# The four sums of weight blocks of each Strassen pair: from VectorE to GpSimd

## The chip, the cores and the metric

The kernel runs on one core of a Trainium2 chip. The metric is device time in microseconds (us), the median of several executions. TensorE (PE in the profile) multiplies matrices, VectorE (DVE), ScalarE (ACT) and GpSimd (POOL) compute element by element, and SyncE (SP) issues most DMAs. Each engine works through its own queue in a fixed order: an instruction that waits holds up everything behind it on its engine.

## The reference, cut to what matters

One decoder layer on 256 tokens of width 2048 in float32: a mixer, a cross-attention, a SwiGLU feed-forward part of width 5632, and norms. Only the last part is touched:

```
def swiglu(h, w_gate, w_up, w_down):
    return (jax.nn.silu(h @ w_gate) * (h @ w_up)) @ w_down
...
        h = h + swiglu(rmsnorm(h, norm_ffn[i]), w_gate[i], w_up[i], w_down[i])
    return rmsnorm(h, norm_final)
```

## The kernel before, in words

**Chunks.** All weights stream through the core once, in one order (`plan`), in chunks of 128 partitions x 1024 elements: two blocks of 128 rows by 512 columns side by side. SP loads a chunk into one of 6 raw tiles (`r`, line 185). ACT rounds it to a high part `h` (line 224, 4 tiles), DVE subtracts to get a low part `l` (line 225, 4 tiles). PE multiplies with both: each product is three matmuls, high x high, low x high and high x low (lines 298, 299, 302). So PE is fed by a chain of load, ACT cast, DVE subtraction, and an `h` tile is free for the next chunk when PE has used it.

**Strassen pairs.** Some chunks are taken two at a time. The first, `g`, and the second, `u`, form a 2 x 2 arrangement of weight blocks, and with a 2 x 2 arrangement of activation blocks the product takes seven block products in place of eight (`seven_mm`, lines 1179, 1180, 1182). For it `pair_sums` makes four sums of weight blocks (lines 199 to 202). Line 199 adds the first halves of `g` and `u`, line 200 changes the first half of `u` in place, line 201 reads the result of 199, and line 202 reads that of 201 and overwrites the first half of `g`, so it must also wait until ACT and DVE have split `g`. Three of the results are then split into high and low parts as well (line 206 on ACT, line 207 on DVE); the fourth is the changed half of `u`, which is split with the rest of `u` on lines 224 and 225.

There are 28 pairs: 16 in the gate and up products (about 813 to 1147 us of the profile), 6 in the first half of the down product (1252 to 1345 us) and 6 in its second half (1359 to 1460 us). Within a part four to six ordinary chunks stand between two pairs. The sums of activation blocks for the down pairs (`token_sums`, lines 1155 to 1160, split on 1165 and 1166) are also made by DVE and ACT, some time ahead.

**What sets the order.** PE's and SP's instructions stand as the code is written. DVE's, ACT's and GpSimd's are put in order when the kernel is built, by a scheduler that goes by its own estimates of how long each instruction takes; so an edit to one instruction can move others in the queues of all three. `split_to` is called up to two chunks ahead of what PE is given.

Of the kernel before, what the change touches and what calls it, by code (L numbers as in the profile page):

```python
# [20 lines left out]
ALU = mybir.AluOpType  # L21
# [100 lines left out]
def trunk(tc, wst, vecs, xp, xtp, mp, mtp, wdt_in, nfin, outp):  # L122
# [9 lines left out]
    with ExitStack() as ctx:  # L132
# [18 lines left out]
        def nm(s):  # L151
            cnt[0] += 1
            return f"{s}{cnt[0]}"

        def slot(shape=(128, 512), dt=F32):
            return sp.tile(list(shape), dt, tag="s", name=nm("s"))
# [12 lines left out]
        tt = nc.vector.tensor_tensor  # L169
        ts = nc.vector.tensor_scalar  # L170
        stt = nc.vector.scalar_tensor_tensor
        gtt = nc.gpsimd.tensor_tensor
# [20 lines left out]
        def pair_sums(key, u):  # L193


            g = held.pop(key)
            a, b = slice(0, 512), slice(512, 1024)
            f = bp.tile([128, 1024], F32, tag="b", name=nm("b"))
            tt(f[:, a], g[:, a], u[:, a], ALU.add)  # L199
            tt(u[:, a], u[:, a], u[:, b], ALU.add)  # L200
            tt(f[:, b], f[:, a], u[:, b], ALU.add)
            tt(g[:, a], f[:, b], g[:, b], ALU.add)  # L202
            pair_parts[key] = []
            for x in (f[:, a], f[:, b], g[:, a]):
                h, l = slot(dt=F32R), slot(dt=F32R)
                nc.scalar.copy(h, x)  # L206
                tt(l, x, h.bitcast(F32), ALU.subtract)  # L207
                pair_parts[key].append((h, l))

        def split_to(n):  # L210
            while nsplit[0] < min(n, len(plan)):
                i = nsplit[0]
                key, w = plan[i]
                r = raws.pop(i)
                if key in first_of:
                    held[key] = r
                elif key in second_of:
                    pair_sums(second_of[key], r)
                h = hip.tile([128, 1024], F32R, tag="h", name=nm("h"))
                l = lop.tile([128, 1024], F32R, tag="l", name=nm("l"))  # L220
                m = 2 if i in (0, 2) else 1
                for j in range(m):
                    c = slice(j * w // m, (j + 1) * w // m)
                    nc.scalar.copy(h[:, c], r[:, c])  # L224
                    tt(l[:, c], r[:, c], h[:, c].bitcast(F32), ALU.subtract)  # L225
                los[i] = l
                his[i] = h
                nsplit[0] += 1
# [1261 lines left out]
```

## Time and profile before

| | before |
|---|---|
| median of 3 runs | 1490.93 us (1490.48 to 1491.18) |
| the profiled execution | 1491.33 us, span of its instructions 1489.6 us |
| PE busy | 1478.4 us, 99% |
| DVE busy | 1109.9 us, 75%, 1528 instructions |
| ACT busy | 829.6 us, 56% |
| GpSimd busy | 34.4 us, 2%, 46 instructions, nearly all before 550 us |
| mean granted TensorE clock | 0.999 |

The span runs from the first instruction to the last, and the execution's own time is 1.7 us more. A busy PE says that matmuls were in flight, and here they follow each other without a gap through the feed-forward part.

### The profile page before, as it was taken

The numbers are of one execution on the slowest core, as the hardware profiler recorded it, in microseconds if no ns is written. First come the engines' busy times: TensorE is split into PE (matmuls) and PEld (weight loads), VectorE is DVE, ScalarE is ACT, GpSimd is POOL, SyncE is SP. The second block draws the span as 40 slices with busy tenths as digits, with TensorE's granted clock in tenths as the row PEclk, the third lists the DMA queues.
The fourth block names the chain that finished last, engine by engine and source line by source line (L and its number), as shares of the span: only waits on it lengthen the run. The fifth ranks groups of instructions, "written<-read, shape, count | busy, mean of one in ns | idle before, by whom it ended". The sixth has DMA issues, their size and how long they took to land.

```text
span 1489.6 us, 18607 instructions
## 1 busy us (share of the span) xinstructions
PE 1478.4 (99%) x6649; PEld 1218.6 (82%) x6649; DVE 1109.9 (75%) x1528; ACT 829.6 (56%) x1155; POOL 34.4 (2%) x46
## 2 busy tenths in 40 slices
PE   9999999999999999999999999999999999999997
PEld 7788888888888888888888888888888888888886
DVE  6677777776785774665577788888887667979975
ACT  7476554857664554554465555555554444655553
POOL 0012000100000000000000000000000000000000
PEclk9999999999999999999999999999999999999999
DMA  9886766868767665876647676756766666765553
GB/s 368 267 286 223 279 214 221 292 223 303 241 212 275 217 233 193 283 274 213 249 166 236 239 242 205 245 204 209 238 226 241 225 220 198 242 217 194 202 187 110
DMA packets 149214, 346.71 MB, mean 233 GB/s; under 512 B 11360, under 2 KB 62976, under 8 KB 149120
## 3 DMA queue, kind: packets, MB, share of 16 engines
q1 hardware_dynamic: 140064, 338.64, 66.1%
q10 hardware_dynamic: 9056, 6.87, 1.5%
q8 instruction: 52, 0.85, 0.2%
q14 instruction: 42, 0.34, 0.1%
HBM read 321.30 MB, written 24.17 MB: 232 GB/s over the span
## 4 chain that ended last, share of the span: by engine, by line
PE 98%; DMA 0%; issue 0%; SPq 0%; ACT 0%; DVE 0%; DVEq 0%; POOLq 0%; POOL 0%
PE a L298 29%; PE a L299 29%; PE a L302 29%; PE m L1182 2%; PE m L1180 2%; PE m L1179 2%; PE a L1179 1%; PE a L1182 1%; PE a L1180 1%; PE m L719 1%; PE m L299 0%; PE m L298 0%; PE m L302 0%; DMA r<-in_w_dram 0%; PE m L1026 0%
## 5 line engine op out<-in xcount | busy, mean ns | idle before, releaser
L225 DVE TENSOR_TENSOR l<-r,h 128x1024 fp32r<-128x1024 f32 (+1 forms) x539 | 652.4, 1218 | 262.3 <-ACT h L224 253.0
L224 ACT CAST h<-r 128x1024 fp32r<-128x1024 f32 (+1 forms) x539 | 563.4, 1049 | 488.1 <-PE a L299 349.3
L298 PE MATMUL a<-h,s 128*128 128x512 f32 x1887 | 738.2, 391 | 1.0 <-ACT h L224 1.0
L299 PE MATMUL a<-h,s 128*128 128x512 f32 x1887 | 734.5, 389 | 0.0
L302 PE MATMUL a<-l,s 128*128 128x512 f32 x1887 | 507.4, 389 | 0.0
L298 PEld LDWEIGHTS a<-h,s 128*128 128x128 f32 x1887 | 354.3, 188 | 76.5 <-ACT h L224 2.1
L302 PEld LDWEIGHTS a<-l,s 128*128 128x128 f32 x1887 | 354.2, 188 | 73.8
L299 PEld LDWEIGHTS a<-h,s 128*128 128x128 f32 x1887 | 354.4, 188 | 72.6
L206 ACT CAST s<-b 128x512 fp32r<-128x512 f32 x56 | 33.9, 619 | 21.0 <-DVE b L199 17.2
L317 DVE STREAM_TRANSPOSE b<-s 128x512 f32<-128x512 f32 x62 | 40.6, 690 | 6.4 <-ACT s L324 6.4
L207 DVE TENSOR_TENSOR s<-b,s 128x512 fp32r<-128x512 f32 x56 | 37.9, 687 | 0.0
L660 DVE SCALAR_TENSOR_TENSOR t<-t,vec,t 128x255 f32<-128x255 f32 (+2 forms) x72 | 33.1, 492 | 3.4 <-ACT t L657 2.7
L199 DVE TENSOR_TENSOR b<-r,r 128x512 f32<-128x512 f32 x28 | 19.3, 689 | 17.3 <-DMA r<-in_w_dram 17.2
L324 ACT ACTIVATE s<-a,xr 128x512 f32<-128x512 f32 x42 | 26.4, 681 | 3.6 <-PE a L302 3.6
L1116 DVE TENSOR_TENSOR f<-a,f 128x512 f32<-128x512 f32 x32 | 20.6, 685 | 8.4 <-PE a L302 8.4
L1143 ACT CAST s<-f 128x512 fp32r<-128x512 f32 x22 | 13.6, 620 | 18.0 <-DMA f<-w 18.0
L1182 PE MATMUL m<-s,t 128*128 128x512 f32 x56 | 21.8, 389 | 0.0
L1179 PE MATMUL m<-s,t 128*128 128x512 f32 x56 | 21.8, 389 | 0.0
L1180 PE MATMUL m<-s,t 128*128 128x512 f32 x56 | 21.8, 389 | 0.0
L206 ACT CAST s<-r 128x512 fp32r<-128x512 f32 x28 | 17.3, 619 | 6.5 <-DVE r L202 6.3
L200 DVE TENSOR_TENSOR r<-r 128x512 f32<-128x512 f32 x28 | 19.3, 689 | 0.4
L207 DVE TENSOR_TENSOR s<-r,s 128x512 fp32r<-128x512 f32 x28 | 19.2, 686 | 0.4 <-ACT s L206 0.4
(232 smaller groups left out, 996.7 us busy)
## 6 DMA issues: line engine op xcount, KB each, us to landing
r<-in_w_dram SPq DMA_DIRECT2D x535, 512.0 KB, 4.6
w<-b SPq DMA_DIRECT2D x42, 512.0 KB, 3.3
f<-w SPq DMA_DIRECT2D x42, 512.0 KB, 5.1
s<-acsT ACTq DMA_DIRECT2D x24, 256.0 KB, 5.2
s<-in_xt_dram SPq DMA_DIRECT2D x16, 256.0 KB, 7.1
s<-in_mt_dram SPq DMA_DIRECT2D x8, 256.0 KB, 6.3
s<-in_m_dram SPq DMA_DIRECT2D x8, 256.0 KB, 4.7
s<-in_x_dram SPq DMA_DIRECT2D x7, 256.0 KB, 7.4
```

What stands on the lines that cost most here:

```text
L206: nc.scalar.copy(h, x)
L207: tt(l, x, h.bitcast(F32), ALU.subtract)
L224: nc.scalar.copy(h[:, c], r[:, c])
L225: tt(l[:, c], r[:, c], h[:, c].bitcast(F32), ALU.subtract)
L298: mm(ps[tb], ah, h[:, w], start=first and i == ks[0], stop=False)
L299: mm(ps[tb], al, h[:, w], start=False, stop=False)
L302: mm(ps[tb], blocks(i, tb)[0], l[:, i * 512:i * 512 + 512], start=False, stop=stop and i == ks[-1])
L317: nc.vector.transpose(t[:, tb * 512:tb * 512 + 512], src[tb])
L660: stt(a[:, d:], u[:, 0:T - d], v("cw", 4 * ct + k), a[:, d:], ALU.mult, ALU.add)
L1179: mm(ps, ah, bh, start=any(ps is q for q in start), stop=False)
L1180: mm(ps, al, bh, start=False, stop=False)
L1182: mm(ps, ah, bl, start=False, stop=any(ps is q for q in stop))
```

## The change

The four sums are issued on GpSimd (`gtt`) in place of DVE (`tt`). Their operands, tiles and number (28 x 4 = 112, each 128 x 512 float32, two inputs) stay. The casts and subtractions of lines 206 and 207 stay on ACT and DVE.

```
             f = bp.tile([128, 1024], F32, tag="b", name=nm("b"))
-            tt(f[:, a], g[:, a], u[:, a], ALU.add)
-            tt(u[:, a], u[:, a], u[:, b], ALU.add)
-            tt(f[:, b], f[:, a], u[:, b], ALU.add)
-            tt(g[:, a], f[:, b], g[:, b], ALU.add)
+            gtt(f[:, a], g[:, a], u[:, a], op=ALU.add)
+            gtt(u[:, a], u[:, a], u[:, b], op=ALU.add)
+            gtt(f[:, b], f[:, a], u[:, b], op=ALU.add)
+            gtt(g[:, a], f[:, b], g[:, b], op=ALU.add)
```

PE's queue is the same instruction for instruction. DVE's loses the 112 sums, and around every pair the scheduler also puts the instructions that are left in another order. Three places matter below. The first is DVE at the second pair of the down product (near 1265 us before). In the names, `r_10924` is `g`, `r_10940` is `u`, `b_11006` holds two of the sums, `f_11112`, `f_11230` and `f_11402` are sums of activation blocks for later pairs, `r_10976` and `r_10980` are ordinary chunks. First before, then now:

```order
L225 TENSOR_TENSOR l_11003<-r_10924,h_11002 128x1024
L199 TENSOR_TENSOR b_11006<-r_10924,r_10940 128x512
L1157 TENSOR_TENSOR f_11112<-f_11112 128x128
L200 TENSOR_TENSOR r_10940<-r_10940 128x512
L201 TENSOR_TENSOR b_11006<-b_11006,r_10940 128x512
L1144 TENSOR_TENSOR s_10995<-f_10954,s_10994 128x512
L202 TENSOR_TENSOR r_10924<-b_11006,r_10924 128x512
L1144 TENSOR_TENSOR s_10999<-f_10954,s_10998 128x512
L225 TENSOR_TENSOR l_11024<-r_10940,h_11023 128x1024
L207 TENSOR_TENSOR s_11012<-b_11006,s_11011 128x512
L225 TENSOR_TENSOR l_11067<-r_10976,h_11066 128x1024
L207 TENSOR_TENSOR s_11016<-b_11006,s_11015 128x512
```

In this fence stands DVE's queue at the same place now, from the second sum of activation blocks on, as far as the first subtractions of the pair:

```order
L1160 TENSOR_TENSOR f_11230<-f_11230 128x128
L225 TENSOR_TENSOR l_11024<-r_10940,h_11023 128x1024
L1144 TENSOR_TENSOR s_10995<-f_10954,s_10994 128x512
L1166 TENSOR_TENSOR t_11119<-f_11112,t_11118 128x256
L225 TENSOR_TENSOR l_11067<-r_10976,h_11066 128x1024
L1144 TENSOR_TENSOR s_10999<-f_10954,s_10998 128x512
L1166 TENSOR_TENSOR t_11123<-f_11112,t_11122 128x256
L207 TENSOR_TENSOR s_11012<-b_11006,s_11011 128x512
L1155 TENSOR_TENSOR f_11402<-s_8195,s_8196 128x512
L207 TENSOR_TENSOR s_11016<-b_11006,s_11015 128x512
L225 TENSOR_TENSOR l_11071<-r_10980,h_11070 128x1024
L207 TENSOR_TENSOR s_11020<-r_10924,s_11019 128x512
```

All eight of lines 1157 to 1160 on the two sums `f_11112` and `f_11230` now stand ahead of `u`'s subtraction `l_11024`, seven more than before, and two of line 1166 and one of line 1155 now stand ahead of the pair's last subtraction `s_11020`.

The second place is ACT's queue at that same pair, as a difference:

```order
 L224 CAST h_11002<-r_10924 128x1024
+L224 CAST h_11023<-r_10940 128x1024
 L1143 CAST s_10994<-f_10954 128x512
-L224 CAST h_11023<-r_10940 128x1024
+L1165 CAST t_11118<-f_11112 128x256
+L224 CAST h_11066<-r_10976 128x1024
 L1143 CAST s_10998<-f_10954 128x512
-L224 CAST h_11066<-r_10976 128x1024
+L1165 CAST t_11122<-f_11112 128x256
 L206 CAST s_11011<-b_11006 128x512
```

`u`'s cast `h_11023`, which needs the second sum, moved up one place, and two casts of activation sums (line 1165) moved ahead of the pair's casts on line 206.

The third place is DVE at the second pair of the second half of the down product (near 1380 us before); `r_11933` is `g` and `r_11949` is `u`. Before:

```order
L225 TENSOR_TENSOR l_12000<-r_11933,h_11999 128x1024
L207 TENSOR_TENSOR s_12013<-b_12003,s_12012 128x512
L202 TENSOR_TENSOR r_11933<-b_12003,r_11933 128x512
L1159 TENSOR_TENSOR f_12107<-f_12107 128x128
L1160 TENSOR_TENSOR f_12107<-f_12107 128x128
L225 TENSOR_TENSOR l_12021<-r_11949,h_12020 128x1024
L207 TENSOR_TENSOR s_12017<-r_11933,s_12016 128x512
```

And now, from the same subtraction of `g` on:

```order
L225 TENSOR_TENSOR l_12000<-r_11933,h_11999 128x1024
L1160 TENSOR_TENSOR f_12397<-f_12397 128x128
L1155 TENSOR_TENSOR f_12515<-s_8199,s_8200 128x512
L1157 TENSOR_TENSOR f_12515<-f_12515 128x128
L1159 TENSOR_TENSOR f_12515<-f_12515 128x128
L1158 TENSOR_TENSOR f_12515<-f_12515 128x128
L225 TENSOR_TENSOR l_12021<-r_11949,h_12020 128x1024
L207 TENSOR_TENSOR s_12017<-r_11933,s_12016 128x512
```

By this point DVE has made the activation sums `f_12225`, `f_12397` and most of `f_12515`, which before it made after `s_12017`.

## The prediction

> **What bounds the kernel now.** I read the page first, then the stretches of the feed-forward part, then the waits, then single places in the timeline. The page:
>
> ```profile
> span 1489.6 us, 18607 instructions
> PE 1478.4 (99%) x6649; PEld 1218.6 (82%) x6649; DVE 1109.9 (75%) x1528; ACT 829.6 (56%) x1155; POOL 34.4 (2%) x46
> PE 98%; DMA 0%; issue 0%; SPq 0%; ACT 0%; DVE 0%; DVEq 0%; POOLq 0%; POOL 0%
> ```
>
> PE is busy nearly all the span and the chain of waits runs through it alone. The stretches (length, then busy time of PE, weight load, DVE, ACT, GpSimd) say the same for the part that is edited, and show how full DVE is there:
>
> ```profile
> 875.00:1136.00 261.00, 261.00 (x1153) 216.19 (x1152) 222.34 (x272) 140.65 (x168) 0.00 (x0) 1.00 0.67 230
> 1262.00:1276.00 14.00, 14.00 (x63) 11.63 (x62) 13.56 (x22) 8.23 (x11) 0.00 (x0) 1.00 0.95 305
> 1276.00:1290.00 14.00, 14.00 (x63) 11.59 (x63) 14.00 (x27) 8.97 (x13) 0.00 (x0) 1.00 0.52 178
> 1350.00:1452.00 102.00, 102.00 (x452) 84.49 (x451) 88.40 (x129) 56.40 (x75) 0.00 (x0) 1.00 0.60 202
> ```
>
> PE has no gap in any of them. So taking work off DVE there can give nothing back: DVE is not what PE waits for. The change can only cost, and it costs where a part of a weight reaches PE later than PE asks for it. The question is how much lead each part has, and how much of it a sum on GpSimd eats. DVE is 85% busy in the gate and up products (222.34 of 261) and 97 to 100% at the start of the down product.
>
> **What a sum costs on DVE and on GpSimd.** The four sums before, 28 of each, and the subtraction of a whole chunk:
>
> ```profile
> L199 DVE TENSOR_TENSOR b<-r,r 128x512 f32<-128x512 f32 x28 | 19.3, 689 | 17.3 <-DMA r<-in_w_dram 17.2
> L202 DVE TENSOR_TENSOR r<-b,r 128x512 f32<-128x512 f32 x28 | 19.3, 688 | 0.2
> L225 DVE TENSOR_TENSOR l<-r,h 128x1024 fp32r<-128x1024 f32 (+1 forms) x539 | 652.4, 1218 | 262.3 <-ACT h L224 253.0
> ```
>
> GpSimd adds nothing of this size before. Its nearest work is the masks of the mixer, which read one tile (shortest, median and longest in ns), and at one place the mixer shows them beside DVE's subtractions:
>
> ```profile
> L629 POOL TENSOR_SCALAR_AFFINE_SELECT s<-s x16: 406/509/1492, 79.4 to 361.2; 128x256 f32<-128x256 f32 x16
> L633 POOL TENSOR_SCALAR_AFFINE_SELECT s<-s x8: 637/820/1616, 80.7 to 359.3; 128x512 f32<-128x512 f32 x8
> 124.49 2.79 DVE L225 TENSOR_TENSOR l<-r,h 128x1024 fp32r<-128x1024 f32 x2 [0.38 <-ACT h L224]
> 125.64 1.65 DVE L225 TENSOR_TENSOR l<-r,h 128x1024 fp32r<-128x1024 f32 x1
> 125.39 0.82 POOL L633 TENSOR_SCALAR_AFFINE_SELECT s<-s 128x512 f32<-128x512 f32 x1 [1.55 <-DMA s<-acsT]
> 126.17 1.39 POOL L629 TENSOR_SCALAR_AFFINE_SELECT s<-s 128x256 f32<-128x256 f32 x1
> ```
>
> Two things are in these rows. Alone, 256 more elements cost 637 - 406 = 231 ns with one input, so 128 x 512 with two inputs should take 637 + 2 x 231 = 1.10 us (estimate), against 0.69 on DVE; the floor is the one-input 0.64. And the two engines take turns. The first subtraction ends at 125.72 (124.49 + 1.22); the mask on line 633 ends 0.49 after that; the second subtraction, issued at 125.64, takes 1.65 in place of 1.22, 0.43 more; and the next mask (0.41 alone) takes 1.39 and ends 0.27 after the second subtraction. Each waits for the other's whole instruction, in strict alternation, when DVE reads two tiles from SBUF. So each sum on GpSimd will hold DVE up by about 0.9 us: 0.43 for one input, twice that for two. Bounds: 0.43 below, 1.1 above (the whole instruction).
>
> The Trainium skill, page "SBUF — State Buffer", section "Who interferes with whom", has this as an exclusive lock between GpSimd and a DVE instruction with two SBUF inputs: the later one blocks until the earlier one ends, and the page measured about 115 ns on top. The trace agrees in kind (0.43 us for a mask of 0.64 that had partly gone by). By that rule a turn would be about 1.2 us and the sum below about 7 us in place of 3.2.
>
> **The gate and up products: hidden.** One of the 16 pairs, the one that PE starts at 1015 (last input landed, two subtractions, PE's uses of them):
>
> ```profile
> 1004.38 0.69 DVE L199 TENSOR_TENSOR b<-r,r 128x512 f32<-128x512 f32 x1 [1.28 <-DMA r<-in_w_dram]
> 1010.27 1.22 DVE L225 TENSOR_TENSOR l<-r,h 128x1024 fp32r<-128x1024 f32 x1
> 1013.94 0.68 DVE L207 TENSOR_TENSOR s<-r,s 128x512 fp32r<-128x512 f32 x1
> 1017.36 0.39 PE L1182 MATMUL m<-l,t 128*128 128x512 f32 x1
> 1019.40 0.39 PE L1182 MATMUL a<-s,s 128*128 128x512 f32 x1
> ```
>
> `u`'s low part is done at 1011.49 and used at 1017.36; the pair's last part is done at 1014.62 and used at 1019.40: 5.9 and 4.8 us of lead. DVE loses 4 x 0.605 = 2.42 us of sums (0.605 is the distance from one start to the next when DVE runs without a break, 1265.38 to 1265.99 below) and is held up 4 x 0.9 = 3.6: 1.2 us later, 2.0 at the upper bound. Covered. The chain through GpSimd is covered too: at worst each sum waits out one subtraction (1.13) and takes 1.1, so four end 8.9 after the landing, at 1013.3, and cast (0.62) and subtraction (0.69) follow by 1014.6. What hides it is that lead; it would be gone if a sum took over about 3.3 us. ACT's casts on line 206, which wait for GpSimd, hold back the casts of line 224 queued behind them by the same 1 to 2 us, within a lead of more than 5. SP waits for raw tiles to be released by these subtractions, so loads go out 1 to 2 us later; a tile is reused six chunks on, and no such delay adds up while DVE has 15% of its time free.
>
> **The down product, second pair: late.** DVE at this pair, and PE's use of its last part:
>
> ```profile
> 1257.25 0.89 SPq L185 DMA_DIRECT2D r<-in_w_dram  x2
> 1262.85 0.69 DVE L1155 TENSOR_TENSOR f<-s,s 128x512 f32<-128x512 f32 x1
> 1263.45 1.22 DVE L225 TENSOR_TENSOR l<-r,h 128x1024 fp32r<-128x1024 f32 x1
> 1265.38 0.69 DVE L200 TENSOR_TENSOR r<-r 128x512 f32<-128x512 f32 x1
> 1265.99 0.69 DVE L201 TENSOR_TENSOR b<-b,r 128x512 f32<-128x512 f32 x1
> 1273.59 0.69 DVE L207 TENSOR_TENSOR s<-r,s 128x512 fp32r<-128x512 f32 x1 [0.44 <-ACT s L206]
> 1275.33 0.29 DVE L1158 TENSOR_TENSOR f<-f 128x128 f32<-128x128 f32 x1
> 1275.53 0.28 DVE L1159 TENSOR_TENSOR f<-f 128x128 f32<-128x128 f32 x1
> 1276.13 0.42 DVE L1166 TENSOR_TENSOR t<-f,t 128x256 fp32r<-128x256 f32 x1
> 1276.47 0.29 DVE L1158 TENSOR_TENSOR f<-f 128x128 f32<-128x128 f32 x1
> 1262.00 1.06 ACT L224 CAST h<-r 128x1024 fp32r<-128x1024 f32 x1 [1.44 <-PE a L299]
> 1275.13 0.39 PE L1182 MATMUL a<-s,s 128*128 128x512 f32 x1
> ```
>
> The last subtraction ends at 1274.28 and PE uses it at 1275.13: a lead of 0.85, with DVE idle for 0.44 in the 11 us before. The new order puts ahead of it work that stood behind: seven of lines 1157 to 1160 (0.20 each, 1275.33 to 1275.53), two of line 1166 (0.34 each) and one of line 1155 (0.60), together 1.40 + 0.68 + 0.60 = 2.68. Out go 2.42 of sums, in come 4 x 0.9 = 3.6 of turns; the idle 0.44 is used up, and `g`'s subtraction at 1263.45 can start when its cast ends, 1263.06, since the first pair's sums, whose inputs landed long before, no longer stand in DVE's way at 1252: 0.39 won. 1274.28 + 2.68 - 2.42 + 3.6 - 0.44 - 0.39 = 1277.3, so PE waits 2.2 us. With turns of 0.43 it is 0.3, with 1.1 it is 3.0. The inputs are there in time (loads issued at 1257.25 and 1257.8). ACT's queue is late as well by the two casts of line 1165 put ahead, but ends within 1 us of PE's need, so DVE decides.
>
> **The down product, second half: late by less.** DVE runs from 1357 to 1383 with one break of 0.21:
>
> ```profile
> 1357.64 1.22 DVE L225 TENSOR_TENSOR l<-r,h 128x1024 fp32r<-128x1024 f32 x1
> 1375.10 0.69 DVE L199 TENSOR_TENSOR b<-r,r 128x512 f32<-128x512 f32 x1 [0.21 <-DMA r<-in_w_dram]
> 1381.80 1.22 DVE L225 TENSOR_TENSOR l<-r,h 128x1024 fp32r<-128x1024 f32 x1
> 1388.69 0.39 PE L1182 MATMUL m<-l,t 128*128 128x512 f32 x1
> ```
>
> Two pairs lie in it. Up to `u`'s subtraction of the second (ends 1383.02, used at 1388.69) eight sums go out, 4.84; three of line 1155, eleven of 1157 to 1160 and two of 1166 move ahead, 1.8 + 2.2 + 0.7 = 4.7; eight turns come in, 7.2; the break gives 0.21 back. It ends at 1389.9, 1.2 late; I take 1.0, since some turns fall beside DVE work that reads PSUM (0 with turns of 0.43, 2.6 with 1.1).
>
> The first down pair has hardly any lead, but for another reason: its sums stood in DVE's queue behind work that waits for PE.
>
> ```profile
> 1232.29 5.76 SPq L185 DMA_DIRECT2D r<-in_w_dram  x3
> 1252.21 0.65 DVE L199 TENSOR_TENSOR b<-r,r 128x512 f32<-128x512 f32 x1
> r<-in_w_dram SPq DMA_DIRECT2D x535, 512.0 KB, 4.6
> ```
>
> Its two chunks are among three loads issued by 1238; at 4.6 us a load they are there by 1243, so GpSimd makes its sums some 9 us before DVE did, while DVE is half idle: it gains lead. The other nine down pairs have leads of 3 to 8 us, and PE's own waiting at the second pair helps those that follow it.
>
> **The sum.** 2.2 + 1.0 = 3.2 us; every other part of the edit costs nothing that reaches PE. The profiled execution took 1491.33, of which 1489.6 is span; the median of the runs is 0.4 less. So 1490.93 + 3.2 = 1494.1, range of this case 1491.9 to 1497.
>
> **Rivals.** *All hidden:* if DVE slips several short instructions between GpSimd's turns, or a turn holds it 0.35 us or less, both places come out in time: 1490.9. For it: the leads elsewhere. Against: the strict alternation at 125 us. A chance of 0.27. *The gate and up pairs stall too:* the turns are longer than the rows say, or ACT's queue, held by a cast that waits for GpSimd, passes the delay on from pair to pair. It decides when a sum takes about 3.3 us; at 0.5 us for each of 16 pairs it adds 8 to the 3.2: 1502. For it: turns of 1.4 and 1.5 us were seen for masks. Against: 15% of free DVE time. 0.25 with everything above 1497. *Faster:* the 112 sums leave DVE 77 us, and if some wait of PE that the stretches don't show ended on DVE, as at the kernel's end, it would shorten: at most a microsecond or three, 1488. Against: PE is full throughout. 0.03.
>
> **Chances.** 0.45 for the sum above, 0.27, 0.25 and 0.03. 0.2% is 3 us, about what a measurement of this kernel can tell from no change. Half of the likeliest case (0.24) lies beyond it, with 0.25 from the longer case and a little more for 0.52 slower; 0.45 same; 0.03 faster. For 8 in 10 the range runs from all hidden, 1490.4, to the gate and up case, 1502.
>
> **What would show it.** In the changed profile: GpSimd near 160 us busy or more, with sums over 1.1 us; L225 means well above 1218; PE idle in 1262 to 1290 and near 1388, and nowhere else in the feed-forward part, with waits on line 1182 released by DVE line 207 and 225. PE full there would show the first rival, gaps at 875 to 1136 the second. I am wrong if GpSimd's turn isn't what the masks show, or if loads, not DVE, come late.

## The result, and the profile after

The changed kernel takes 1511.31 us (median of 3 runs, 1511.31 to 1515.25) against 1490.93 before: ratio 1.0144, 95% interval 1.0131 to 1.0158. It is 20.4 us slower, where 3.2 were predicted and 11 allowed for. The profiled execution is the one of 1515.25 us, 23.9 us of span longer than the profiled one before, so the places below add up to that.

The page after, in the order in which the page before was read:

```profile
span 1513.5 us, 18736 instructions
PE 1487.8 (98%) x6649; PEld 1220.8 (81%) x6649; DVE 1091.8 (72%) x1416; ACT 820.0 (54%) x1155; POOL 203.0 (13%) x158
PE 4%; issue 1%; DVE 1%; DMA 1%; POOL 1%; ACT 1%; POOLq 0%; DVEq 0%; ACTq 0%; SPq 0%
L225 DVE TENSOR_TENSOR l<-r,h 128x1024 fp32r<-128x1024 f32 (+1 forms) x539 | 667.6, 1255 | 258.8 <-ACT h L224 249.9
L199 POOL TENSOR_TENSOR b<-r,r 128x512 f32<-128x512 f32 x28 | 37.5, 1340 | 407.4 <-DMA r<-in_w_dram 370.6
L207 DVE TENSOR_TENSOR s<-b,s 128x512 fp32r<-128x512 f32 x56 | 52.3, 936 | 41.3 <-ACT s L206 41.3
L202 POOL TENSOR_TENSOR r<-b,r 128x512 f32<-128x512 f32 x28 | 46.5, 1661 | 115.2 <-issue 71.5
```

Followed back from its end, the chain reaches only as far as 1375 us, so its shares add up to a tenth of the span; in that stretch it no longer runs through PE alone. DVE lost 112 instructions of 0.69 us, yet is only 18 us less busy (1109.9 to 1091.8), because those that stay got longer: the subtraction of a chunk (L225) went from 1218 to 1255 ns on the mean, a subtraction of a pair's sums (L207) from 687 to 936. The stretches that were shown before (length, then PE, weight load, DVE, ACT, GpSimd, granted clock):

```profile
875.00:1136.00 261.00, 259.25 (x1139) 213.19 (x1138) 210.54 (x220) 134.86 (x164) 66.03 (x48) 1.00 0.62 219
1262.00:1276.00 14.00, 14.00 (x64) 11.59 (x63) 12.11 (x12) 5.15 (x6) 6.22 (x4) 1.00 0.92 299
1276.00:1290.00 14.00, 11.54 (x50) 8.91 (x49) 13.87 (x28) 8.46 (x13) 2.29 (x2) 1.00 0.52 184
1350.00:1452.00 102.00, 95.32 (x410) 77.21 (x409) 76.58 (x104) 48.03 (x68) 28.47 (x19) 0.98 0.54 186
```

PE has gaps in the gate and up products and in both halves of the down product. What they waited for, by the view of waits for PE over the feed-forward part (total, times, longest):

```profile
PE m L1182 <- DVE l L225: 4.8, 3, 2.6
PE a L298 <- ACT h L224: 3.5, 2, 2.1
PE a L1179 <- DVE g L1133: 2.1, 1, 2.1
PE m L1182 <- DVE s L207: 1.6, 1, 1.6
PE a L1179 <- DVE f L1116: 1.6, 3, 0.6
PE a L1182 <- DVE s L207: 0.8, 1, 0.8
PE a L302 <- DVE l L225: 0.4, 1, 0.4
```

That is 14.8 us of waiting. Counted as distance from one matmul's start to the next beyond the usual 0.227 us, PE lost 23.5: a slow clock behind three of the gaps is in that (below).

### The profile page after: what moved, and what is told of

The parts are those of the page before. It is cut to its first block, busy times and chain, and to the rows that moved or that the text cites. A ratio compares the mean times of both kernels' runs of the same rounds, so it can differ in the third digit from the quotient of the medians.

```text
span 1513.5 us, 18736 instructions
## 1 busy us (share of the span) xinstructions
PE 1487.8 (98%) x6649; PEld 1220.8 (81%) x6649; DVE 1091.8 (72%) x1416; ACT 820.0 (54%) x1155; POOL 203.0 (13%) x158
## 5 line engine op out<-in xcount | busy, mean ns | idle before, releaser
L225 DVE TENSOR_TENSOR l<-r,h 128x1024 fp32r<-128x1024 f32 (+1 forms) x539 | 667.6, 1255 | 258.8 <-ACT h L224 249.9
L224 ACT CAST h<-r 128x1024 fp32r<-128x1024 f32 (+1 forms) x539 | 555.3, 1045 | 352.7 <-PE a L299 297.6
L206 ACT CAST s<-b 128x512 fp32r<-128x512 f32 x56 | 34.7, 619 | 109.4 <-POOL b L199 86.1
L199 POOL TENSOR_TENSOR b<-r,r 128x512 f32<-128x512 f32 x28 | 37.5, 1340 | 407.4 <-DMA r<-in_w_dram 370.6
L207 DVE TENSOR_TENSOR s<-b,s 128x512 fp32r<-128x512 f32 x56 | 52.3, 936 | 41.3 <-ACT s L206 41.3
L202 POOL TENSOR_TENSOR r<-b,r 128x512 f32<-128x512 f32 x28 | 46.5, 1661 | 115.2 <-issue 71.5
L278 POOL TENSOR_TENSOR rr<-rv,half 128x2 f32<-128x2 f32 x8 | 6.5, 812 | 409.5 <-DVE rv L277 409.5
L201 POOL TENSOR_TENSOR b<-b,r 128x512 f32<-128x512 f32 x28 | 45.3, 1620 | 0.0
L206 ACT CAST s<-r 128x512 fp32r<-128x512 f32 x28 | 17.4, 621 | 47.5 <-POOL r L202 47.5
L200 POOL TENSOR_TENSOR r<-r 128x512 f32<-128x512 f32 x28 | 38.4, 1373 | 2.2
L1144 DVE TENSOR_TENSOR s<-f,s 128x512 fp32r<-128x512 f32 x22 | 18.9, 868 | 23.8 <-ACT s L1143 23.0
L629 POOL TENSOR_SCALAR_AFFINE_SELECT s<-s 128x256 f32<-128x256 f32 x16 | 10.4, 658 | 169.6 <-DMA s<-acsT 119.7
L207 DVE TENSOR_TENSOR s<-r,s 128x512 fp32r<-128x512 f32 x28 | 19.1, 683 | 15.9 <-ACT s L206 15.9
```

Source lines behind the costliest of these rows:

```text
L199: gtt(f[:, a], g[:, a], u[:, a], op=ALU.add)
L200: gtt(u[:, a], u[:, a], u[:, b], op=ALU.add)
L201: gtt(f[:, b], f[:, a], u[:, b], op=ALU.add)
L202: gtt(g[:, a], f[:, b], g[:, b], op=ALU.add)
```

## The experiments

Medians in us; the kernel before ran beside each of them (1491.1 to 1491.4), and the ratio is to it. "Taken" is what GpSimd's turns took from DVE by busy time: DVE's busy time less that of the kernel with the same DVE instructions and no add on GpSimd. (The expectations quote 53, 82 and 118 us for three of these. They sum how much longer each DVE instruction is than the median of its kind, which counts the overlap of neighbours twice.) Where PE has gaps, the executions of one kernel spread by up to 4.7 us (deep_raw, 1507.75 to 1512.49), so a difference of 2 us between two such kernels means little.

| label | GpSimd does | median | ratio, 95% interval | taken |
|---|---|---|---|---|
| changed kernel | 4 sums of each pair | 1511.31 | 1.0144 (1.0131 to 1.0158) | 44.7 |
| gate_up_only | the sums of 16 pairs | 1496.15 | 1.0035 (1.0023 to 1.0047) | |
| down_only | the sums of 12 pairs | 1507.38 | 1.0106 (1.0089 to 1.0123) | |
| subs_too | sums and L207 | 1564.33 | 1.0493 (1.0477 to 1.0509) | |
| dummy_adds | unread adds beside DVE's sums | 1553.22 | 1.0415 (1.0400 to 1.0431) | 109.3 |
| no_sums | nothing, sums left out | 1491.34 | 1.0002 (0.9992 to 1.0011) | 0 |
| holds_only | unread adds, sums left out | 1513.76 | 1.0156 (1.0141 to 1.0172) | 70.7 |
| holds_half | the same, half as wide | 1493.63 | 1.0016 (1.0006 to 1.0025) | 30.6 |
| waits_only | 2 memsets for each sum | 1491.01 | 1.0000 (0.9991 to 1.0009) | -0.6 |
| waits_long | 4 memsets for each sum | 1491.05 | 0.9998 (0.9989 to 1.0008) | 1.9 |
| parts_late | sums; L206, L207 issued later | 1510.55 | 1.0136 (1.0119 to 1.0152) | |
| extra_on_dve | nothing; 6 more adds on DVE | 1511.26 | 1.0128 (1.0111 to 1.0145) | |
| first_two | L199, L200 | 1493.09 | 1.0010 (1.0001 to 1.0019) | |
| first_only | L199 | 1491.56 | 1.0002 (0.9993 to 1.0012) | |
| deep_raw | 4 sums, 7 raw tiles | 1511.47 | 1.0130 (1.0115 to 1.0145) | |
| spare | the sums of 25 pairs | 1501.98 | 1.0074 (1.0057 to 1.0091) | |

**Where.** One part of the change at a time:

```
-            gtt(f[:, a], g[:, a], u[:, a], op=ALU.add)
+            (tt if key[0] == "d" else gtt)(f[:, a], g[:, a], u[:, a], op=ALU.add)   # gate_up_only; the other three alike
+            (gtt if key[0] == "d" else tt)(f[:, a], g[:, a], u[:, a], op=ALU.add)   # down_only
```

> The sums of the 16 gate/up pairs on GpSimd, those of the 12 down pairs on DVE as before. In the changed kernel PE lost 6.8 us in the gate/up part (five gaps at L1179, released by DVE's L1116 and L1133) and 16.7 us in the down product. If the two parts lose time independently, this kernel loses the first alone: 1490.9 + 7 = 1498, between 1496 and 1500, with gaps at the same five places and none after 1140 us. Rival: DVE's load of the whole feed-forward part matters (work put off in the gate/up part is still owed in the down product): then the down product loses time here as well, 1502 or more.

> The mirror image: the sums of the 12 down pairs on GpSimd, those of the 16 gate/up pairs on DVE. Independent parts: 1490.9 + 16.7 = 1507.6, between 1505 and 1511, no gap before 1250 us. Rival (debt carried over from the gate/up part): under 1503.

5.1 and 16.3 us, together 21.4 where the whole change costs 20.4: to within 1 us the two parts lose on their own, and nothing is seen to be owed from one to the other. Twelve pairs of the down product cost three times what sixteen pairs of the gate and up products do.

**Turn or wait.** Two things are new for DVE: it takes turns with GpSimd, and it waits for GpSimd's results. The first two kernels put more of the one than of the other:

```
-                tt(l, x, h.bitcast(F32), ALU.subtract)
+                gtt(l, x, h.bitcast(F32), op=ALU.subtract)          # subs_too
```
```
# dummy_adds: the kernel before, with slots at 62 and behind the sums
+            z = dummy.tile([128, 512], F32, tag="z", name=nm("z"))
+            for _ in range(4): gtt(z, g[:, b], u[:, b], op=ALU.add)
```

> GpSimd makes the four sums of each pair and the three subtractions L207 too, so that no instruction on DVE waits for GpSimd any more; GpSimd has 84 more instructions (196 in all). Queue theory (DVE works in order and stood at an L207 whose sum GpSimd had not finished, with the evacuations L1116 and L1133 behind it): the gaps of the gate/up part at L1179 go, 6.8 us less there; in the down product the parts themselves come later by three GpSimd instructions, so the losses there stay or grow. 1503 to 1512, the gate/up part with under 1 us lost. Hold theory (each instruction of GpSimd holds DVE by a turn of about 1.1 us, whoever waits): 84 more turns, the gaps of the gate/up part stay or grow beyond 6.8 us, 1513 to 1530.

> The sums on DVE as before, and beside them GpSimd adds the second halves of the same two raw tiles four times for each pair into a tile that nobody reads (112 instructions of the same kind and size; the slots pool has 62 tiles in place of 63 to make room). Nothing waits for GpSimd's results but the release of the raw tiles; DVE's order stays nearly that of the kernel before. Hold theory: DVE has the 112 sums and the 112 turns of about 1.1 us, so its splits and evacuations are later than in the changed kernel: 1510 or more. Queue theory: 1491 to 1496, no gap of the gate/up part; DVE's instructions beside GpSimd's lengthen all the same (L225 mean above 1.25 us).

The queue theory, which I held after reading the changed profile, failed in both by 50 us and more; the hold theory had the sign of both and was 34 us short in the first. subs_too isn't a clean test, though: 16.3 of the 47.9 us that PE waits there are for parts that GpSimd itself subtracted (L207), so it has a longer chain as well as more turns. What it does show is that the gaps at L1179 stay (8.7 us of waits) when no instruction on DVE waits for GpSimd directly (ACT's copies still do, and DVE's subtractions wait for ACT). In dummy_adds, adds whose result nobody reads cost 62 us, three times the change. At one pair of its gate and up products (timeline of GpSimd, then of DVE; its lines 197 to 199 are lines 199 to 201 elsewhere, its line 202 the unread adds):

```profile
1002.00 7.00 POOL L202 TENSOR_TENSOR z<-r,r 128x512 f32<-128x512 f32 x4 [13.81 <-DMA r<-in_w_dram]
1002.14 1.78 DVE L197 TENSOR_TENSOR b<-r,r 128x512 f32<-128x512 f32 x1
1003.95 1.67 DVE L198 TENSOR_TENSOR r<-r 128x512 f32<-128x512 f32 x1
1005.54 2.31 DVE L225 TENSOR_TENSOR l<-r,h 128x1024 fp32r<-128x1024 f32 x1
1007.78 1.77 DVE L199 TENSOR_TENSOR b<-b,r 128x512 f32<-128x512 f32 x1
```

Four adds, and four instructions of DVE each 1.0 to 1.1 us longer than alone (0.69 and 1.22): strict alternation. The next four take the two apart without DVE's own sums in the way:

```
# no_sums, holds_only: sums out, the parts are split from raw blocks
-            for x in (f[:, a], f[:, b], g[:, a]):
+            for x in (g[:, a], u[:, a], g[:, b]):
# holds_only, in place of the sums
+            for x in (f[:, a], f[:, b], f[:, a], f[:, b]): gtt(x, g[:, b], u[:, b], op=ALU.add)
# waits_only, in place of the sums (waits_long: four memsets)
+            for x in (f[:, a], u[:, a], f[:, b], g[:, a]):
+                nc.gpsimd.memset(x, 0.001)
+                nc.gpsimd.memset(x, 0.002)
```

> Leaves the four sums of each pair out: the three extra parts are split from the raw blocks g[:, a], u[:, a] and g[:, b]. DVE has the changed kernel's 1416 instructions, GpSimd 46 as before, and nothing waits for a sum. Both theories: no gap of PE, 1490.5 to 1491.5. It is the base of the next run, which has the same order on DVE, ACT, PE and SP, row by row.

> The kernel without sums, and GpSimd makes four adds of the raw blocks' second halves for each pair into the tile f, which nobody reads: the changed kernel's 112 instructions, of the same kind and size, at the same places, with nobody waiting for their results (the release of the raw tiles and of f apart). Hold theory (what costs is that each of these instructions takes a turn of up to 1.1 us from DVE): most of the changed kernel's 20 us, 1503 to 1511. Wait theory (what costs is that ACT's copies L206, and through them DVE's subtractions L207 with all that is queued behind them, wait for GpSimd's chain of four): under 1495.

> Each of the four sums on GpSimd is replaced by two memsets of the same block (a sum is left out, its place in the chain and who waits for it stays): about 1.2 us of GpSimd for each, near the 1.29 us of a sum that runs alone (estimate from L425, 0.31 us for half a block). If a memset takes no turn from DVE, DVE's L225 keep 1.22 us, and what is lost is lost to the waits alone: the wait theory says 1503 to 1511, the hold theory under 1495. If L225 lengthens beside the memsets, this run tells nothing apart.

> As the run with two memsets for each sum (1491.0 us, nothing lost, DVE's L225 unchanged at 1.224 us), but four memsets of 0.53 us for each sum: a chain of 8.4 us for a pair where the changed kernel's took 6.0 (1.34 + 1.37 + 1.62 + 1.66). The copies L206 then wait at least as long for GpSimd as in the changed kernel (156 us in all; with two memsets only 4 us). Turn theory (waits alone cost nothing while the leads of 4 to 8 us hold, the turns make the loss): under 1494. Rival (the waits were only too short in the last run, and a chain as long as the changed kernel's loses by itself): 1500 or more.

no_sums and holds_only have the same order on every engine but GpSimd, and 112 unread adds make 22.4 us between them. That this is so near the changed kernel's 20.4 is in part chance: the gate and up part loses 3.8 us here in place of 6.8, none of it in waits for L1116 or L1133, and the gaps of the down product stand elsewhere. The memsets make nothing. Groups of waits_long, DVE's subtraction and two of GpSimd's:

```profile
L225 DVE TENSOR_TENSOR l<-r,h 128x1024 fp32r<-128x1024 f32 (+1 forms) x539 | 653.1, 1219 | 314.5 <-ACT h L224 307.2
L200 POOL MEMSET r<- 128x512 f32 x224 | 117.3, 527 | 375.0 <-DMA r<-in_w_dram 216.1 <-DVE l L225 108.6 <-ACT h L224 23.1
L200 POOL MEMSET b<- 128x512 f32 x224 | 107.8, 528 | 66.1 <-DMA w<-b 34.8 <-DVE s L207 17.0 <-DVE l L225 13.8
```

GpSimd is busier here than in the changed kernel (257.5 us against 203.0) and L225 is at its 1.22 us: an instruction that only writes takes no turn here. The Trainium skill has this as a rule, page "SBUF — State Buffer", section "Who interferes with whom": a DVE instruction with two SBUF inputs contends with a GpSimd instruction that reads SBUF, not with one that only writes it, and a DVE instruction with at most one SBUF input, outside DVE's two-port modes, does not contend. The second half agrees as well: in holds_only 27 instructions of lines 1096 to 1099, one of whose two inputs is in PSUM (the memory of PE's accumulators), overlapped an add and took 0.68 us on the mean (0.69 at most), as alone. Three limits of these runs. First, L206 waited 30 us in all for the long memsets, not the 156 of the changed kernel that I expected: without turns both sides kept pace. So waits of that size have no run of their own; a chain of 8.4 us for each pair loses nothing, and adds whose results nobody reads lose as much as the change. Second, these adds still hold their raw tiles: two gaps of holds_only, at 1413 and 1421, with 9.9 of the 21.7 us that PE loses in its profile, stand behind loads that went out late (last section). Third, no run has the changed kernel's order on DVE and ACT without GpSimd's adds, so what the new order costs by itself is not measured.

**How much a turn takes, and how many are free.**

> The kernel that leaves the sums out and has four unread adds for each pair on GpSimd (1513.8 us, 82 us taken from DVE in turns of up to 1.11 us), with adds half as wide (128x256): the same 112 instructions, the same order on all engines. If a turn lasts as long as GpSimd's instruction, DVE's excess falls to at most half (under 45 us, no single one above 0.6 us), and since leads absorb the first part of it the loss falls by more than half: 1491 to 1497. If a turn has a fixed price whatever the width: 1508 or more.

> Only the first two sums of each pair (L199, L200) on GpSimd, the others on DVE: 56 turns in place of 112, and DVE keeps 38 us of sums. If the loss goes with the number of turns alone: half, near 1501. If leads absorb a first part: 1491 to 1497. If DVE's sums that wait for GpSimd's (L201 for L199) bring stalls of their own: above 1503.

> Only the first sum of each pair (L199) on GpSimd: 28 turns. With 56 turns 1493.1, with 112 turns 1511.3: leads take up the first turns, so this should be 1491 to 1492, no gap of PE longer than 1 us. 1495 or more would say that each turn has a price of its own.

holds_half writes `x[:, 0:256]` from `g[:, 512:768]` and `u[:, 512:768]`. The turn is half as long (DVE's instructions at most 0.60 us longer, against 1.12) and takes 30.6 in place of 70.7 us, but the loss falls from 22.4 to 2.3 us. With one, two and four sums of each pair on GpSimd it is 0.2, 1.8 and 20.4 us. So turns of some 30 us, spread over the pairs, are nearly free. What more turns cost isn't given by their amount: 44.7 us of them go with a loss of 20.4 in the changed kernel (23.9 in the execution that was profiled), 70.7 with 22.4 in holds_only.

**Amount or placement.** `for _ in range(6): tt(z, g[:, b], u[:, b], ALU.add)` in dummy_adds' place:

> The sums on DVE as before, and six further adds for each pair on DVE itself (raw second halves into a tile that nobody reads): 168 instructions of 0.69 us, 116 us, as much as the 112 turns took from DVE in the run with unread adds on GpSimd beside sums on DVE (118 us; 1553 us). Amount theory (DVE time is lost, in whatever form): the same loss of 50 to 70 us, 1540 to 1560. Placement theory (turns fall on whatever DVE does while GpSimd works, urgent splits too, while DVE's own adds stand where the order of the instructions has room for them): much less, 1491 to 1520.

Six more adds of DVE's own make it 92 us busier (1202.1 less 1109.9) and cost 20 us; the turns of dummy_adds took 109 and cost 62. So DVE's time is dear by itself once the leads are gone, and a turn is dearer. That it falls on whatever DVE does while GpSimd works would explain this; it is argued, not shown, for the two kernels differ in DVE's order too.

**Who hands it on.**

```
# parts_late: copies and subtractions of a pair are issued after the next chunk's split
+            late.append((key, (f[:, a], f[:, b], g[:, a])))
...
                his[i] = h
+                if due: late_parts()
# deep_raw
-        rawp = E(tc.tile_pool(name="raw", bufs=6))
+        rawp = E(tc.tile_pool(name="raw", bufs=7))
# spare, for the four sums
+            (tt if key in (("d", 0, 1), ("d", 2, 0), ("d", 2, 1)) else gtt)(f[:, a], g[:, a], u[:, a], op=ALU.add)
```

> The sums on GpSimd as in the changed kernel, but the copies L206 and subtractions L207 of a pair's three parts are issued one raw chunk later (after the next chunk's own split), so that ACT and DVE come to them when GpSimd is done. Wait theory: the five gaps of the gate/up part at L1179 go (6.8 us) and some of the down product's 16.7 us, unless the parts are then too late for PE there: 1493 to 1506. Hold theory: the turns stay, so do the losses: 1508 to 1515.

> The changed kernel with seven raw tiles in place of six (and 61 slots in place of 63 to make room), so that a load waits for the release of the seventh tile back. In the changed kernel the loads of the down product's second half stop for 6 us (issued at 1400.5 and next at 1406.8), since DVE is late with the raw tiles, and PE's two last gaps (1419 and 1455, 4 us and a slow clock behind the second) follow from the data that land late. If late loads carry these, they go: 5 us or more back, 1503 to 1507, the other gaps unchanged. If the loads are only a sign of DVE's lateness and DVE is what PE waits for anyway: 1509 to 1513.

> Three pairs of the down product (the second of its first half, the first and the second of its second half), the ones with a gap of PE at their own products, have their sums on DVE again; the other 25 stay on GpSimd. If each pair's loss is its own: the gaps at 1282, 1284, 1384, 1388 and 1407 go, 10 us, 1500 to 1503, the gate/up part's 6.8 us unchanged. If DVE's lateness is handed on from pair to pair: the gaps move to other pairs and less than 5 us come back.

parts_late takes most of the loss out of the gate and up part. Its waits there (its lines 1186, 1122 and 1139 are lines 1179, 1116 and 1133 elsewhere):

```profile
PE a L1186 <- DVE f L1122: 0.7, 1, 0.7
PE a L1186 <- DVE g L1139: 0.5, 1, 0.5
```

1.2 us against 3.7. But the whole is hardly faster, 19.5 us over the kernel before in place of 20.4; in the down product PE's gaps stand at other places (the longest, 2.5 us, at 1323, where the changed kernel has 0.4). Of the 8.5 us that PE waits there, 7.4 are for ACT's casts of ordinary chunks (L224 elsewhere). A later place in the order lets DVE pass the wait in the gate and up part; whether turns or waits delay those casts is not separated. With seven raw tiles the last two gaps shrink to one of 1.0 us, so late loads did carry them; but new gaps of 3.0 and 2.4 us open at 1305 and 1344 and the whole is no faster. That run also has two slots fewer and another order on DVE, so where the new gaps come from stays open. Sparing three pairs gives 9.3 us back, close to the 10 that their own gaps held: pairs lose mostly each by itself.

## Why the prediction was wrong

What held: time given back to DVE is worth nothing here (no_sums has DVE 63 us less busy than before and 1491.34 us), so the change could only cost; the mechanism, the two engines taking turns; and the second pair of the down product, its place and its size. DVE there, then the last subtraction before PE's use at 1284.94:

```profile
1268.58 3.49 DVE L1155 TENSOR_TENSOR f<-s,s 128x512 f32<-128x512 f32 x2
1271.99 2.32 DVE L225 TENSOR_TENSOR l<-r,h 128x1024 fp32r<-128x1024 f32 x1
1274.63 1.37 DVE L1158 TENSOR_TENSOR f<-f 128x128 f32<-128x128 f32 x1
1284.20 0.68 DVE L207 TENSOR_TENSOR s<-r,s 128x512 fp32r<-128x512 f32 x1
```

The step "each sum on GpSimd will hold DVE up by about 0.9 us" was mis-sized, in both directions. Here it was short. The two of the first row take 1.78 us each where 0.69 is usual, the subtraction 2.32 for 1.22, the small one 1.37 for 0.28: a full turn is 1.1 us, my upper bound, since GpSimd's add takes 1.29 us alone where I estimated 1.10. Nothing on top of the add's own length is seen. With 1.1 the prediction's own sum gives 3.0 us at this pair, as measured. Over the whole it was far too long: 112 sums took 44.7 us from DVE, 0.40 each, and only 64 DVE instructions were slowed. So DVE as a whole was held up less than predicted, and the loss was still six times the forecast: it came from places without lead, and from waits. By place (PE's loss by start to start, the slow clock included):

| place | predicted | measured | PE released by |
|---|---|---|---|
| gate and up products | 0 | 6.8 | DVE L1133, L1116 |
| second pair of the first half | 2.2 | 3.0 | DVE L207 |
| at 1328 and 1365 | 0 | 1.1 | ACT L224, DVE L225 |
| first pair of the second half | 0 | 5.5 | DVE L225 |
| second pair of the second half | 1.0 | 1.5 | DVE L225 |
| after it, 1419 and 1456 | 0 | 5.6 | ACT L224 |

**"The gate and up products: hidden" is the step that failed first.** I weighed the leads of weight parts and of nothing else. PE also waits for DVE to empty a PSUM accumulator (L1133, L1116), and that had a lead of only 2.0 us at the first pair: before, the first L1133 ended at 827.04 and PE wrote at 829.00.

```profile
813.24 0.69 DVE L199 TENSOR_TENSOR b<-r,r 128x512 f32<-128x512 f32 x1 [3.74 <-DMA r<-in_w_dram]
822.81 0.69 DVE L202 TENSOR_TENSOR r<-b,r 128x512 f32<-128x512 f32 x1
826.30 1.40 DVE L1133 SCALAR_TENSOR_TENSOR g<-a,fscale,g 128x512 f32<-128x512 f32 x2
829.00 0.39 PE L1179 MATMUL a<-h,t 128*128 128x512 f32 x1
```

There, now, on GpSimd, ACT, DVE and PE:

```profile
813.53 1.29 POOL L199 TENSOR_TENSOR b<-r,r 128x512 f32<-128x512 f32 x1 [26.66 <-DMA r<-in_w_dram]
817.92 0.62 ACT L206 CAST s<-b 128x512 fp32r<-128x512 f32 x1 [2.45 <-POOL b L201]
825.34 2.14 POOL L202 TENSOR_TENSOR r<-b,r 128x512 f32<-128x512 f32 x1 [7.46 <-issue]
827.52 0.62 ACT L206 CAST s<-r 128x512 fp32r<-128x512 f32 x1 [2.62 <-POOL r L202]
828.17 0.69 DVE L207 TENSOR_TENSOR s<-r,s 128x512 fp32r<-128x512 f32 x1 [1.83 <-ACT s L206]
829.12 1.23 DVE L225 TENSOR_TENSOR l<-r,h 128x1024 fp32r<-128x1024 f32 x1 [0.25 <-ACT h L224]
830.26 1.40 DVE L1133 SCALAR_TENSOR_TENSOR g<-a,fscale,g 128x512 f32<-128x512 f32 x2
831.06 0.52 PE L1179 MATMUL a<-h,t 128*128 128x512 f32 x1 [2.08 <-DVE g L1133]
```

GpSimd's last sum starts 2.5 us later than DVE's did and takes 2.14 us, with a subtraction's turn in it. It starts late because it needs `g` split: ACT stood 2.45 us at its copy for GpSimd's third sum, so the cast behind it ran at 822.90 in place of 820.47, and the subtraction that the last sum waits for ended at 825.20. The prediction let four sums end 8.9 us after the landing at worst, without this wait; from the first one's start they took 10.3 us on DVE and 13.9 on GpSimd. Then ACT and DVE wait for the last sum one after the other, and the emptying of the accumulator, which waited for nothing of this pair, stands behind them in DVE's queue and comes 4.0 us later than before: 2.0 beyond its lead. DVE stood idle for 6.3 us between 816.7 and 830.3, so what costs at this pair is more the waiting than the turns. The rival in which the gate and up pairs stall I had priced at 1502 with a chance of 0.25; one of its two mechanisms, ACT's queue held by a cast that waits for GpSimd, is what is seen, but its condition, a sum of over 3.3 us, was not met: the longest took 2.3.

**"The other nine down pairs have leads of 3 to 8 us"** failed at the second half. I gave the first pair there no row of its own, and it lost most. "No such delay adds up", which I said of the gate and up products, does not hold here: at the last gaps the delays add up. The chain of waits up to the gap at 1419 (start, length, what):

```profile
1407.51 1.15 DVE l L225
1408.68 4.36 DMA r<-in_w_dram
1413.20 1.26 POOL b L199
1414.49 0.63 ACT s L206
1416.30 1.52 DVE t L1166
1418.08 1.05 ACT h L224
```

DVE is late to free a raw tile, the load goes out late, GpSimd's sums are late, a subtraction beside them (L1166) takes 1.52 us with a turn in it, ACT stands 2.14 us at its second copy, up to 1417.56, and a cast of an ordinary chunk that PE needs (L224) stands behind that.

**The clock** is the third miss. Stretches of 3 us behind four gaps of the changed kernel (the seventh number is the granted clock):

```profile
831.10:834.50 3.40, 3.40 (x9) 2.71 (x10) 3.40 (x5) 1.04 (x1) 0.00 (x0) 0.55 0.40 151
1282.10:1285.00 2.90, 2.07 (x9) 1.38 (x9) 2.90 (x5) 1.26 (x3) 0.00 (x0) 1.00 0.32 120
1388.30:1391.40 3.10, 3.10 (x8) 2.49 (x9) 3.10 (x5) 1.45 (x2) 0.00 (x0) 0.53 0.90 289
1455.80:1459.20 3.40, 3.40 (x10) 2.57 (x10) 3.40 (x4) 2.84 (x3) 0.00 (x0) 0.54 0.42 124
```

Behind gaps of 2.25, 2.8 and 2.2 us PE ran at about half clock for some 3 us, 0.43 us for a matmul in place of 0.23, some 4.8 us in all; behind one of 1.8 us it did not. So these three gaps, 7.3 us in all, cost two thirds as much again, which no term of my sum had.

## What to carry to other kernels

Where two engines take turns at memory, moving work from one to the other does not take all of its time off the first: the sums were 63 us of DVE's time, and 45 came back as turns, up to 1.1 us for an instruction that had cost 0.69 and falling on whatever DVE was doing. When you ask whether a delay is covered, list everything that the bound engine waits for, the emptying of its accumulators as well as its inputs, and take the shortest lead in each queue behind the delayed instruction. Test a move with work that nobody reads first: it gives a price without the wait for the results, though its operands are still held.

## What the runs showed of the hardware

The turn can go the other way. At one place of holds_only DVE runs without a break, and GpSimd is the one that starves; two adds and DVE's last two subtractions in their time:

```profile
1388.28 16.11 POOL L199 TENSOR_TENSOR b<-r,r 128x512 f32<-128x512 f32 x2 [11.93 <-DMA r<-in_w_dram]
1399.63 2.36 DVE L225 TENSOR_TENSOR l<-r,h 128x1024 fp32r<-128x1024 f32 x2
```

The first add took 14.9 us in place of 1.29, to 1.2 us after DVE's run had ended, while DVE's instructions beside it kept their length. It holds its raw tiles so long that the next loads go out late, and 9.9 us of that run's loss, at 1413 and 1421, stand behind them. In dummy_adds at 1002 DVE had no break either, and there the two alternated; what decides between the two is not settled here.

Nor is the length of a gap alone what halves the clock: 2.34 us at 1411 in down_only did not, 2.47 us at 1448 in the same run did. Over the feed-forward parts of all these traces no gap of up to 1.93 us was followed by a slow stretch, every one from 2.47 us on was, and those between went either way (1.95 us in parts_late did, 2.44 in spare did not).

```profile
1411.20:1414.60 3.40, 3.40 (x16) 2.79 (x17) 3.40 (x4) 2.95 (x4) 0.00 (x0) 1.00 0.38 143
1447.80:1451.20 3.40, 3.40 (x9) 2.68 (x10) 3.40 (x4) 2.93 (x4) 0.00 (x0) 0.53 0.36 125
```

The Trainium skill, page "TensorE: Matmul & The Clock Gate", section "Part 1: The HAM clock gate (the "warmup" mystery)", has a free-running window of about 3.4 us, after an idle one of which the clock is halved. The slow stretches of the changed kernel, 2.7 to 3.7 us from PE's restart, are near one window, and a window that doesn't start with the gap would explain that like gaps end differently; but here gaps of 1.95 to 2.8 us were enough, shorter than the window.
